# A Hymba-style layer in fp32 on one core: the S5 output matmuls as a task of their own, weights split three chunks ahead in the input projection, accumulators loaded one by one, and another root and other stores at the end

## The chip, the cores and the metric

The kernel runs on one core of a Trainium2 chip. The metric is the device time of one launch in microseconds (us); lower is better. Three runs of the kernel before took 2394.06 to 2394.51 us, with a median of 2394.2 us.

## The reference, cut to what matters

One layer is applied to 656 columns: 16 meta tokens, 512 prompt tokens and 8 streams of 16 sample tokens. Everything is fp32.

```python
hn = rmsnorm(x, g_mix);  proj = hn @ w_in              # 2048 -> 1024 (S5) + 1024 (pooling)
# S5: 64 groups of 16 channels, 64 complex states each
bu = einsum("gpn,blgn->blgp", b_bar, u);  h = scan(h*lam_bar + bu)
y  = einsum("gnp,blgp->blgn", c, h).real + d_skip * u
y  = gelu(y);  y = y * sigmoid(y @ w_glu)
# pooling: trailing means over 2/4/8/16 positions minus the token, times w_pool, times a scale
x  = x + concat([y, y_pool]) @ w_out
g, v = rmsnorm(x, g_ffn) @ w_up                        # 2048 -> 2 x 5632
x  = x + (gelu(causal_conv3(g)) * v) @ w_down          # 5632 -> 2048
out = rmsnorm(x, g_final)                              # and the final states of S5, pooling and conv
```

## The kernel before, in words

Activations lie channel-first: a tile has 128 channels on the partitions and up to 656 columns. Each fp32 product is made of three fp32r matmuls: the high part of a weight times the high and the low part of the activations, and the low part of the weight times the high part. Weights come from DRAM in chunks of four 128x128 tiles (`wraw`, issued by SP, L197). Each chunk is split into `wh` (a CAST on ACT) and `wl` (a subtraction on DVE), and PE then runs 24 main matmuls over it, each of 320 or 336 columns.

The stages in time, in us from the start of the span: input projection with the S5 and pooling work beside it (0 to about 475, with the first part of the output projection), the GLU matmuls (480 to 552), the rest of the output projection (to 650), the up projection as a Strassen-like scheme (to 1745), the down projection (to 2317), and its tail, which goes through the columns in two pieces of 384 and 256 (`TAIL`), the final RMSNorm and the stores of y.

S5 runs in eight blocks n of eight groups. `prep_b` and `prep_c` build the block's matrices (POOL, ACT and some small fp32 matmuls). `s5(n)` issues the input matmuls into PSUM tiles `vps`, copies them to `vt`, and does complex multiplications, rotations and two scans on DVE, with temporaries `pr` and `cr`. The last sum of a block on DVE is `vt<-pr,vt`. The output matmuls `yps` follow (`ymm`); they read `kst`, `cexp`, `ht` and `vt`. `s5_out(n)` then takes `yps` through gelu on ACT and DVE, stores the block to DRAM (`yg_d`), loads it again in another layout and splits it into the GLU's input `H`. The last block is needed by the first GLU row of weights whose input it is.

The order of instructions is not written by hand. One Python planner emits the instructions of all engines while it builds the program. The main line emits the main matmuls; after each of them `tick` gives background tasks (generators) a turn. A planner clock `E.now` is moved on by modelled matmul costs, and each other engine has such a clock (`Eng.clk`, moved on by a fixed and a per-element cost). A task yields until such clocks have reached what it waits for (`done`, `idle`, `until`), or until a flag of another task is set. On the chip each engine runs its own list in order, and semaphores hold the real dependences. So a planner cost that is off shows as a wait on the chip, because the engine's list is in the wrong order for it.

In the down projection, `feed` loads the hidden tiles (`hidb`, 320 KB each, L1528) and, at the start, the 16 residual tiles into `acc` (L1627). `evict_down` adds each finished PSUM tile (`md`, `me`) to `acc` on DVE. In the tail `fin_acc` adds the last PSUM tile, squares it on ACT, and sums the squares on POOL or DVE. `fin_norm` sums over the partitions with a matmul of ones, takes the reciprocal root as exp(-0.5 ln(s)), does a Newton step on DVE, multiplies, and stores (L1713).

Of the kernel before, what the change touches and what calls it, by code (L numbers as in the profile page):

```python
# [14 lines left out]
NFF = 44  # L15
# [94 lines left out]
class Eng:  # L110
# [3 lines left out]
    def __init__(self, E, eng, fixed, per, fast=None):  # L114
        self.E, self.eng, self.fixed, self.per, self.fast = E, eng, fixed, per, fast
        self.clk = 0.0

    def __getattr__(self, m):
# [12 lines left out]

        return call
# [27 lines left out]
class Emit:  # L160
    def __init__(self, tc, A):
        self.tc, self.nc, self.A = tc, tc.nc, A
        self.order = weight_order()
        self.wi = 0
        self.slot = 0
        self.bg = []
        self.raw = {}
        self.hl = {}
        self.nraw = 0
        self.nh = 0  # L170
        self.nchunk = len(self.order) // CH
# [103 lines left out]
def body(tc, A):  # L275
# [40 lines left out]
    with tc.manual_schedule():  # L316
# [5 lines left out]
        def w26():  # L322
            return sp.tile([128, NT], F32, tag="w26", name="w26", bufs=7)
# [222 lines left out]
        def prep_b(n):  # L546
# [20 lines left out]
            while gbusy[0]:  # L567
                yield
# [56 lines left out]
        def s5(n):  # L625
            q0 = 4 * n
            pr = sp.tile([128, 4, 2, 2, NB], F32, tag="pr", name="pr", bufs=1)
# [9 lines left out]
            S.copy(out=ht[:, :, 0, :, 33:41], in_=h0)  # L637
# [37 lines left out]
            gbusy[0] = False  # L675
# [4 lines left out]
            yield from V.idle()  # L680
            times1(vt[:, :, 1], m2c)
# [30 lines left out]
            yield from V.idle()  # L712
            yps = pps.tile([128, 2, 512], F32, tag="sy", name="yps", bufs=1)

            def ymm(q):
# [8 lines left out]
            times1(ht[:, :, 0], m2c)  # L724
            TT(ht[:, :, 1], vt[:, :, 1], pr[:, :, 0], ADD)
            yield from V.idle()
            yield from times2(ht, m1)
            TT(fl(od), fl(pr), fl(ev), ADD)
            yield from V.done(0.8)
            while not cready[0] > n:  # L730
                yield
            for q in range(4):
                ymm(q)
                if q % 2:
                    yield
# [45 lines left out]
        gbusy = [False]  # L781
# [36 lines left out]
        def s5_main():  # L818
            for n in range(NSSM):
                while bready[0] <= n:  # L820
                    yield
                gbusy[0] = True
# [782 lines left out]
        def feed():  # L1605
# [30 lines left out]

        def evict_down(n, t):
            av = half2(D["acc"][:, n])
# [28 lines left out]
        def fin_acc(n, o, w, p, last):  # L1667
# [5 lines left out]
            if last and n >= 14:  # L1673
                sqt.append(q)
                return
            if last:
                S.activation(out=av, in_=av, func=AF.Copy, scale=vcol(V_GFIN, n))
# [9 lines left out]
        def fin_norm(o, w, last):  # L1687
# [17 lines left out]
            for lo in cuts:  # L1705
                for m in range(lo, hi):
                    av = acc[:, m, o:o + w]
                    if last and m < 14:
                        TT(av, av, rw, MUL, G if m in (3, 6, 9, 12) else V)
                    else:  # L1710
                        STT(av, av, vcol(V_GFIN, m), rw, MUL, MUL)
                yield from V.done(0.1)
                SP.dma_start(out=A["y"][lo:hi, :, o:o + w].rearrange("n p c -> p n c"), in_=acc[:, lo:hi, o:o + w])  # L1713
# [6 lines left out]
        for half, (o, w) in enumerate(TAIL):  # L1720
            for ks, ns in tail_order(half):
# [15 lines left out]
                if half == 1 and ns == [12]:  # L1737
                    S.activation(out=dmy, in_=epst, func=AF.Ln)
            if half == 0:
                first = list(E.bg)  # L1740
# [18 lines left out]
    ("y", (16, 128, 640)), ("sst", (8, 128, 4, 2, 9)), ("pst", (8, 128, 15, 9)), ("cvo", (128, NFF, 2, 9)),  # L1759
# [58 lines left out]
def _gather(o):  # L1818
# [3 lines left out]
    y = o["y"].reshape(2048, 16, 40)  # L1822
# [25 lines left out]
```

## Time and profile before

| what | value |
|---|---|
| median of three runs | 2394.2 us |
| the profiled execution's own time | 2393.66 us |
| its span, first to last instruction | 2391.9 us, mean granted TensorE clock 0.991 |
| PE / PE weight loads busy | 2340.7 us (98%) / 2330.3 us (97%) |
| DVE / ACT / POOL busy | 1646.5 (69%) / 936.5 (39%) / 347.4 us (15%) |
| DMA | 265.93 MB, 111 GB/s on the mean |
| 165 to 270 us: PE, DVE, POOL busy of 105 us | 93.23, 87.42, 54.50 |
| 270 to 375 us | 94.57, 81.31, 40.34 |
| 375 to 480 us | 105.00, 74.02, 31.55 |

PE stands for TensorE's matmuls, DVE for VectorE, ACT for ScalarE, POOL for GpSimd and SP for SyncE, whose queue issues the transfers. The granted clock is a share of full speed: 1.00 is 2.4 GHz and 0.50 is 1.2 GHz.

### The profile page before, as it was taken

How to read it: one execution, taken by the hardware profiler on the slowest of the kernel's cores; microseconds unless marked ns; L12 is line 12 of the kernel's file. 1: busy time of each engine (PE TensorE's matmuls, PEld its weight loads, DVE VectorE, ACT ScalarE, POOL GpSimd, SP SyncE). 2: the span in 40 equal slices, each digit the busy share in tenths (PEclk: the TensorE clock that was granted, in tenths of full speed). 3: DMA queues.
4: the chain of work that ended last, by engine and by line, in shares of the span. 5: the costliest groups of instructions: out<-in, count | busy, mean ns of one | idle time of the engine just before them, and what ended most of it. 6: DMA issues, size and time to landing. Idle time of an engine off the chain costs nothing.

```text
span 2391.9 us, 41092 instructions
## 1 busy us (share of the span) xinstructions
PE 2340.7 (98%) x15824; PEld 2330.3 (97%) x15824; DVE 1646.5 (69%) x2725; ACT 936.5 (39%) x1631; POOL 347.4 (15%) x548
## 2 busy tenths in 40 slices
PE   9998989999999999999999999999999999999997
PEld 9997989999999999999999999999999999999997
DVE  7588677646798888888888888888853232422236
ACT  6233343335554444444444444444441221311124
POOL 5655433200000000000000000000000000000014
PEclk9999899999999999999999999999999999999999
DMA  5322235545533333333323333333473232422223
GB/s 187 113 79 82 81 113 178 159 137 162 165 104 106 92 108 91 99 106 97 108 89 101 100 100 106 92 102 95 115 243 103 86 124 72 135 75 76 72 84 110
DMA packets 151237, 265.93 MB, mean 111 GB/s; under 512 B 21120, under 2 KB 41728, under 8 KB 151040
## 3 DMA queue, kind: packets, MB, share of 16 engines
q1 hardware_dynamic: 144560, 248.10, 33.4%
q0 software_dynamic: 6336, 15.19, 2.2%
q8 instruction: 124, 2.03, 0.4%
q14 instruction: 73, 0.60, 0.1%
q10 hardware_dynamic: 144, 0.01, 0.0%
HBM read 225.10 MB, written 38.12 MB: 110 GB/s over the span
## 4 chain that ended last, share of the span: by engine, by line
PE 75%; DVE 2%; DMA 1%; issue 1%; ACT 0%; SPq 0%; DVEq 0%; POOL 0%; ACTq 0%; POOLq 0%
PE pu L157 44%; PE me L157 12%; PE md L157 12%; PE mm L157 5%; PE mf L157 2%; DVE acc L130 1%; DMA acc<-x_d 1%; DVE f L130 0%; DVE wl L130 0%; DMA hidb<-h_d 0%; DMA h_d<-f 0%; ACT wh L130 0%; DMA wr<-wup 0%; DVE XH L130 0%; SPq L1295 0%
## 5 line engine op out<-in xcount | busy, mean ns | idle before, releaser
L157 PE MATMUL pu<-XT,wh 128*128 128x320 f32 (+1 forms) x3696 | 823.7, 310 | 0.5 <-DVE f L130 0.5
L157 PEld LDWEIGHTS pu<-XT,wh 128*128 128x128 f32 x3696 | 620.3, 188 | 0.9 <-issue 0.7
L157 PE MATMUL pu<-XT,wl 128*128 128x320 f32 (+1 forms) x1848 | 572.2, 310 | 0.7 <-DVE wl L130 0.7
L130 ACT CAST wh<-wraw 128x512 fp32r<-128x512 f32 (+1 forms) x487 | 298.4, 617 | 588.8 <-PE md L157 219.9
L130 ACT CAST wh<-wr 128x512 fp32r<-128x512 f32 x434 | 269.2, 621 | 405.6 <-PE pu L157 252.4
L130 DVE TENSOR_TENSOR wl<-wraw,wh 128x512 fp32r<-128x512 f32 (+1 forms) x487 | 336.4, 705 | 93.3 <-ACT wh L130 89.9
L157 PE MATMUL mm<-H,wh 128*128 128x320 f32 (+2 forms) x1920 | 372.6, 316 | 9.2 <-ACT H L130 4.2
L157 PEld LDWEIGHTS pu<-XT,wl 128*128 128x128 f32 x1848 | 349.2, 189 | 1.4 <-DVE wl L130 1.4
L130 DVE TENSOR_TENSOR wl<-wr,wh 128x512 fp32r<-128x512 f32 x434 | 298.1, 687 | 72.7 <-ACT wh L130 66.9
L157 PEld LDWEIGHTS mm<-H,wh 128*128 128x128 f32 x1920 | 304.4, 190 | 12.2 <-issue 7.1
L157 PE MATMUL pu<-XH,wh 128*128 128x320 f32 (+1 forms) x1232 | 277.1, 310 | 0.0
L157 PE MATMUL mm<-H,wl 128*128 128x320 f32 x960 | 222.4, 313 | 0.0
L157 PEld LDWEIGHTS pu<-XH,wh 128*128 128x128 f32 x1232 | 207.1, 189 | 0.0
L157 PE MATMUL pu<-XH,wl 128*128 128x320 f32 (+1 forms) x616 | 190.3, 309 | 0.0
L130 DVE TENSOR_TENSOR acc<-md,acc 128x640 f32<-128x640 f32 (+2 forms) x48 | 34.0, 710 | 193.9 <-PE md L157 193.9
L157 PEld LDWEIGHTS mm<-H,wl 128*128 128x128 f32 x960 | 163.3, 190 | 0.5 <-DVE wl L130 0.4
L130 DVE TENSOR_TENSOR acc<-me,acc 128x640 f32<-128x640 f32 (+2 forms) x48 | 34.1, 711 | 186.5 <-PE me L157 186.5
L157 PE MATMUL me<-hidb,wh 128*128 128x320 f32 x832 | 157.0, 311 | 5.1 <-ACT wh L130 5.1
L157 PE MATMUL md<-hidb,wh 128*128 128x320 f32 x832 | 156.5, 310 | 0.0
L157 PEld LDWEIGHTS me<-hidb,wh 128*128 128x128 f32 x832 | 131.7, 189 | 5.3 <-ACT wh L130 5.3
L157 PEld LDWEIGHTS md<-hidb,wh 128*128 128x128 f32 x832 | 131.6, 189 | 0.0
L130 DVE TENSOR_TENSOR wr<-wr 128x512 f32<-128x512 f32 x172 | 118.4, 688 | 2.8
(241 smaller groups left out, 3248.6 us busy)
## 6 DMA issues: line engine op xcount, KB each, us to landing
wraw<-wts SPq DMA_DIRECT2D x323, 256.0 KB, 2.8
wr<-wup SPq DMA_DIRECT2D x260, 256.0 KB, 3.0
wraw<-wup SPq DMA_DIRECT2D x90, 256.0 KB, 2.7
h_d<-f POOLq DMA_DIRECT2D x44, 320.0 KB, 2.5
hidb<-h_d SPq DMA_DIRECT2D x30, 320.0 KB, 4.3
w<-yg_d SPq DMA_DIRECT2D x16, 328.0 KB, 3.2
w<-xr SPq DMA_DIRECT2D x16, 322.0 KB, 3.7
x_d<-w SPq DMA_DIRECT2D x16, 322.0 KB, 3.7
```

Of the source, the lines that this page charges most:

```text
L130: return f(*a, **k)
L157: return self.eng.matmul(out=out, lhsT=lhsT, rhs=rhs, start=start, stop=stop, **more)
```

## The change

- Planner: a DVE instruction costs 1.2 times as much in the planner while POOL's planner clock is ahead of it. The small S5 tiles `w26` have 6 buffers where there were 7.
- S5: `pr` has two buffers. The last sum of a block goes to `pr` where it went to `vt`, and the output matmuls read it there. They are now a task, `s5_y(n)`, and `s5_main` goes straight on to block n+1: its input matmuls may stand ahead of block n's output matmuls. The initial state is copied to `ht` only once block n-1's output matmuls are emitted. The flag `gbusy` becomes the counter `g_done`.
- Input projection: at row 3 of four, one more chunk is split, so that from there on weights are split three chunks ahead.
- Down projection: four residual tiles are loaded at the start, and the other twelve by a task, one each 6 us of planner time; `evict_down` is not emitted before its tile's load.
- Tail: `fin_acc` multiplies by `g_final` on ACT in both column pieces. The reciprocal root is a Sqrt on ACT (its table is loaded after the first piece by a small Sqrt), a DVE reciprocal and the Newton step. Each piece is multiplied by five DVE instructions (2, 4, 4, 4 and 2 tiles), none on POOL, and stored by five transfers to an output of its own, where a partition's data of one transfer lies together.

The diff, cut to its core:

```diff
-            self.clk = max(self.clk, self.E.now) + self.fixed + per * n
+            t = max(self.clk, self.E.now)
+            self.clk = t + (self.fixed + per * n) * (1.2 if self.rival and self.rival.clk > t else 1)
...
+        self.V.rival = self.G
...
-            return sp.tile([128, NT], F32, tag="w26", name="w26", bufs=7)
+            return sp.tile([128, NT], F32, tag="w26", name="w26", bufs=6)
...
-            while gbusy[0]:
+            while g_done[0] < n:
...
-            pr = sp.tile([128, 4, 2, 2, NB], F32, tag="pr", name="pr", bufs=1)
+            pr = sp.tile([128, 4, 2, 2, NB], F32, tag="pr", name="pr", bufs=2)
...
-            S.copy(out=ht[:, :, 0, :, 33:41], in_=h0)
...
+            while s5_done[0] < n:
+                yield
+            S.copy(out=ht[:, :, 0, :, 33:41], in_=h0)
             times1(vt[:, :, 1], m2c)
...
             yield from times2(ht, m1)
-            TT(fl(od), fl(pr), fl(ev), ADD)
-            yield from V.done(0.8)
+            TT(fl(pr), fl(pr), fl(ev), ADD)
+            E.spawn(s5_y(n, pr, st))
+
+        def s5_y(n, pr, st):
+            yield from V.done(1.5)
             while not cready[0] > n:
                 yield
+            yps = pps.tile([128, 2, 512], F32, tag="sy", name="yps", bufs=1)
             for q in range(4):
...
-                    T.matmul(out=ov[:, 1:4:2], lhsT=lhs, rhs=vt[:, q, 1:4:2, ri], start=False, stop=ri == 1)
+                    T.matmul(out=ov[:, 1:4:2], lhsT=lhs, rhs=pr[:, q, :, ri], start=False, stop=ri == 1)
...
+                if n == 2 and k == 3:
+                    E.split_hi()
+                    E.split_lo()
...
-            for g in range(16):
-                SP.dma_start(out=half2(D["acc"][:, g]), in_=x3_d[g])
-                if g % 4 == 3:
-                    yield 2
+            for g in range(4):
+                load_acc(g)
+                yield 2
+            E.spawn(rest_acc())
...
+        def rest_acc():
+            t = E.now
+            for g in range(4, 16):
+                yield from E.until(t + 10 + 6 * (g - 4))
+                load_acc(g)
+
         def evict_down(n, t):
+            while n not in accs:
+                E.tick(True)
...
-            S.activation(out=rw, in_=ps[:, 0:w], func=AF.Ln, bias=epst)
+            S.activation(out=rw, in_=ps[:, 0:w], func=AF.Sqrt, bias=epst)
...
-            S.activation(out=rw, in_=rw, func=AF.Exp, scale=-0.5)
-            S.clk += 2.6
-            yield from S.done()
+            yield from S.done(0.2)
+            V.reciprocal(out=rw, in_=rw)
             newton(rw, rw, aw, t2[:, 0:w])
...
-            cuts = (15, 14, 12, 10, 8, 6, 4, 2, 0) if last else tuple(range(14, -1, -2))
...
+            for lo in (14, 10, 6, 2, 0):
+                av = acc[:, lo:hi, o:o + w]
+                TT(av, av, rw.unsqueeze(1).to_broadcast([128, hi - lo, w]), MUL)
                 yield from V.done(0.1)
-                SP.dma_start(out=A["y"][lo:hi, :, o:o + w].rearrange("n p c -> p n c"), in_=acc[:, lo:hi, o:o + w])
+                SP.dma_start(out=A[f"y{int(last)}"][:, lo:hi], in_=av)
                 hi = lo
```

**Places in the order.** PE's list around the output matmuls of block 1 (`yps<-stk,kst` is the first of them; `vps` are the input matmuls of block 2; `mm` are main matmuls). Before:

```order
L157 MATMUL mm<-H_85,wl 128x336
L157 MATMUL yps<-stk,kst 128x164
L157 MATMUL yps<-ht,cexp 128x2x41
L157 MATMUL yps<-vt,cexp 128x2x41
...
L157 MATMUL mm<-H_85,wl 128x336
L157 MATMUL vps<-stk,gst 128x164 x4
L157 MATMUL mm<-H_85,wh 128x320 x2
```

The same place now:

```order
L159 MATMUL mm<-H_85,wl 128x336
L159 MATMUL vps<-stk,gst 128x164 x8
L159 MATMUL mm<-H_0_77,wh 128x320 x2
...
L159 MATMUL mm<-H_2_79,wl 128x336
L159 MATMUL yps<-stk,kst 128x164
L159 MATMUL yps<-ht,cexp 128x2x41
L159 MATMUL yps<-pr,cexp 128x2x41
```

The input matmuls of block 2 moved ahead of the output matmuls of block 1. Counted from the start of the program, 1014 main matmuls stood ahead of the first output matmul of block 1, and 1074 stand there now; for block 2 it is 1248 and 1284, for block 3 1464 and 1524, for block 7 2352 and 2370.

ACT's list around the output of block 7, the last one (`<-yps` reads the output matmuls, the ACTIVATE on a tile onto itself is first the tanh and then the scale by 0.5, `CAST H` splits the reloaded block). Before:

```order
L130 ACTIVATE w_5204<-yps 128x656
L130 CAST wh<-wraw 128x512
L130 ACTIVATE w_5204<-w_5204 128x656
L130 CAST wh<-wraw 128x512 x2
L130 ACTIVATE w_5203<-w_5203 128x656
L130 CAST wh<-wraw 128x512 x2
L130 CAST H_85<-w_5312 128x640
```

The same place now:

```order
L132 ACTIVATE w_5234<-yps 128x656
L132 CAST wh<-wraw 128x512 x2
L132 ACTIVATE w_5234<-w_5234 128x656
L132 CAST wh<-wraw 128x512
L132 ACTIVATE w_5233<-w_5233 128x656
L132 CAST wh<-wraw 128x512
L132 CAST H_85<-w_5348 128x640
```

One weight cast moved from behind the tanh to ahead of it, and the scale now has three casts ahead of it since `yps`, as before, but of chunks that are one later. On DVE the first gelu instruction on this block (a TENSOR_SCALAR) stood ahead of the eviction of the last pooling map (`w<-mm,w` x3) and stands behind it now.

SP's list where the accumulators are loaded. Before:

```order
L1528 DMA hidb<-h_d_150 128x640
L1627 DMA acc<-x_d_126 128x640
...
L1627 DMA acc<-x_d_133 128x640
L197 DMA wraw<-wts 128x512
L1627 DMA acc<-x_d_134 128x640
...
L1627 DMA acc<-x_d_141 128x640
L1528 DMA hidb<-h_d_151 128x640
```

The same place now:

```order
L1534 DMA hidb<-h_d_150 128x640
L1644 DMA acc<-x_d_126 128x640
L1644 DMA acc<-x_d_127 128x640
L200 DMA wraw<-wts 128x512
L1644 DMA acc<-x_d_128 128x640
L1644 DMA acc<-x_d_129 128x640
L1534 DMA hidb<-h_d_151 128x640
...
L1644 DMA acc<-x_d_130 128x640
```

Twelve of the sixteen loads moved behind the hidden tile `h_d_151`.

## Rows read from the trace of the kernel before

**Rows 1.** What PE waited for: times in us in total, count, longest.

```profile
PE yps L157 <- DVE vt L130: 16.5, 4, 6.2
PE me L157 <- ACT wh L130: 5.1, 1, 5.1
...
PE mm L157 <- DVE H L130: 3.3, 1, 3.3
```

**Rows 2.** Windows after five PE waits: PE PEld DVE ACT POOL, clock, DMA, GB/s.

```profile
185.40:192.40 7.00, 7.00 (x39) 7.00 (x40) 5.75 (x10) 0.00 (x0) 2.43 (x4) 0.66 0.45 113
238.30:245.30 7.00, 7.00 (x33) 7.00 (x33) 2.81 (x6) 0.73 (x1) 0.00 (x0) 0.54 0.30 92
287.20:294.20 7.00, 7.00 (x37) 6.94 (x38) 2.83 (x6) 1.31 (x2) 0.00 (x0) 0.62 0.40 112
323.70:330.70 7.00, 7.00 (x39) 7.00 (x40) 6.96 (x13) 1.64 (x4) 5.76 (x10) 0.79 0.74 212
1782.10:1789.10 7.00, 7.00 (x31) 7.00 (x32) 5.33 (x8) 4.26 (x7) 0.00 (x0) 0.61 0.90 307
```

**Rows 3.** Windows of S5 blocks 1 to 3, same columns.

```profile
149.20:185.30 36.10, 29.98 (x203) 28.97 (x201) 35.58 (x57) 11.46 (x23) 22.10 (x23) 0.97 0.25 69
185.30:197.50 12.20, 12.12 (x75) 12.12 (x76) 5.85 (x11) 2.03 (x6) 7.13 (x10) 0.80 0.27 67
197.50:238.30 40.80, 35.23 (x242) 34.65 (x240) 40.21 (x62) 16.32 (x33) 21.76 (x27) 1.00 0.33 95
238.30:251.20 12.90, 12.90 (x75) 12.90 (x76) 2.81 (x7) 2.77 (x7) 4.61 (x6) 0.75 0.16 50
251.20:287.20 36.00, 32.06 (x220) 31.49 (x218) 35.52 (x58) 14.77 (x30) 19.34 (x25) 0.98 0.34 95
```

**Rows 4.** Timeline of DVE, block 1: start, us, instruction.

```profile
172.82 0.16 DVE L130 TENSOR_TENSOR st<-pr 128x4 f32<-128x4 f32 x1
...
182.11 1.77 DVE L130 TENSOR_TENSOR pr<-pr,cr 128x656 f32<-128x656 f32 x1
183.91 1.42 DVE L130 TENSOR_TENSOR vt<-pr,vt 128x656 f32<-128x656 f32 x1
```

**Rows 5.** Groups of PE by form, 290 to 480 us: count, busy, mean ns.

```profile
L157 PE MATMUL vps<-stk,gst 128*128 128x164 f32 x64 | 10.5, 304 | 0.2 <-DVE H L130 0.2
```

**Rows 6.** Timeline of DVE and ACT around block 7's output.

```profile
477.67 0.84 DVE L130 TENSOR_TENSOR w<-w,w 128x656 f32<-128x656 f32 x1
...
480.90 0.95 DVE L130 TENSOR_TENSOR w<-mm,w 128x320 f32<-128x320 f32 x3 [2.39 <-PE mm L157]
...
483.24 0.75 ACT L130 ACTIVATE w<-w 128x656 f32<-128x656 f32 x1 [2.02 <-DVE w L130]
...
484.63 0.62 ACT L130 CAST wh<-wraw 128x512 fp32r<-128x512 f32 x1 [0.64 <-PE mm L157]
488.21 0.62 ACT L130 CAST wh<-wraw 128x512 fp32r<-128x512 f32 x1 [2.96 <-PE mm L157]
...
492.79 0.90 DVE L130 TENSOR_TENSOR H<-w,H 128x640 fp32r<-128x640 f32 x2 [3.23 <-ACT H L130]
```

**Rows 7.** Chain that ended last, 1750 to 1790 us: start, us, what.

```profile
1762.87 6.45 DMA acc<-x_d
...
1775.82 5.62 DMA hidb<-h_d
```

**Rows 8.** Timeline of the last 16 us.

```profile
2377.17 1.28 ACT L130 ACT_TABLE_LOAD   x1
...
2378.46 0.42 ACT L130 ACTIVATE f<-f 128x256 f32<-128x256 f32 x1
...
2380.29 1.35 DVE L130 SCALAR_TENSOR_TENSOR acc<-acc,vec,f 128x256 f32<-128x256 f32 x2
...
2381.56 5.01 DVE L130 TENSOR_TENSOR acc<-acc,f 128x256 f32<-128x256 f32 x10
```

**Rows 9.** Groups of DVE by form, 0 to 60 us.

```profile
L130 DVE RECIPROCAL pt<-pt 128x32 f32<-128x32 f32 x1 | 0.4, 352 | 4.2 <-POOL pt L130 4.2
```

More of the change, by code (lines that the diff above doesn't have):

```diff
@@ L116, in __init__ @@
         self.clk = 0.0
+        self.rival = None
     def __getattr__(self, m):
@@ L674, in s5 @@
                 gmm(q)
-            gbusy[0] = False
+            g_done[0] = n + 1
             yield from S.done(0.4)
@@ L712, in s5 @@
             yield from V.idle()
+            times1(ht[:, :, 0], m2c)
+            TT(ht[:, :, 1], vt[:, :, 1], pr[:, :, 0], ADD)
+            yield from V.idle()
+            yield from times2(ht, m1)
+            TT(fl(pr), fl(pr), fl(ev), ADD)
+            E.spawn(s5_y(n, pr, st))
+        def s5_y(n, pr, st):
+            yield from V.done(1.5)
+            while not cready[0] > n:
+                yield
             yps = pps.tile([128, 2, 512], F32, tag="sy", name="yps", bufs=1)
-            def ymm(q):
+            for q in range(4):
                 o = yps[:, q // 2, 164 * (q % 2):164 * (q % 2) + 164]
@@ L721, in ymm @@
                     T.matmul(out=ov[:, 0:4:2], lhsT=lhs, rhs=ht[:, q, :, ri], start=False, stop=False)
-                    T.matmul(out=ov[:, 1:4:2], lhsT=lhs, rhs=vt[:, q, 1:4:2, ri], start=False, stop=ri == 1)
[L724 to L727, printed above, removed]
-            TT(fl(od), fl(pr), fl(ev), ADD)
-            yield from V.done(0.8)
[L730 to L733, printed above, removed]
+                    T.matmul(out=ov[:, 1:4:2], lhsT=lhs, rhs=pr[:, q, :, ri], start=False, stop=ri == 1)
                 if q % 2:
@@ L779, in s5_out @@
             s5_out_done[0] += 1
-        gbusy = [False]
+        g_done = [0]
         cready = [0]
@@ L821, in s5_main @@
                     yield
-                gbusy[0] = True
                 yield from s5(n)
@@ L1635, in body, with load_acc @@
         E.spawn(feed())
+        def load_acc(g):
+            SP.dma_start(out=half2(D["acc"][:, g]), in_=x3_d[g])
+            accs.add(g)
+        accs = set()
+        def rest_acc():
[3 more added lines that the diff above has]
+                load_acc(g)
         def evict_down(n, t):
+            while n not in accs:
+                E.tick(True)
             av = half2(D["acc"][:, n])
@@ L1674, in fin_acc @@
                 sqt.append(q)
+                if n == 15:
+                    for m in (14, 15):
+                        am = acc[:, m, o:o + w]
+                        S.activation(out=am, in_=am, func=AF.Copy, scale=vcol(V_GFIN, m))
                 return
-            if last:
-                S.activation(out=av, in_=av, func=AF.Copy, scale=vcol(V_GFIN, n))
+            S.activation(out=av, in_=av, func=AF.Copy, scale=vcol(V_GFIN, n))
             yield from S.done()
@@ L1695, in fin_norm @@
             rw, aw = r[:, 0:w], a[:, 0:w]
-            S.activation(out=rw, in_=ps[:, 0:w], func=AF.Ln, bias=epst)
+            S.activation(out=rw, in_=ps[:, 0:w], func=AF.Sqrt, bias=epst)
             V.tensor_scalar(out=aw, in0=ps[:, 0:w], scalar1=1e-6, scalar2=None, op0=ADD)
-            S.activation(out=rw, in_=rw, func=AF.Exp, scale=-0.5)
-            S.clk += 2.6
-            yield from S.done()
+            yield from S.done(0.2)
+            V.reciprocal(out=rw, in_=rw)
             newton(rw, rw, aw, t2[:, 0:w])
             yield
-            cuts = (15, 14, 12, 10, 8, 6, 4, 2, 0) if last else tuple(range(14, -1, -2))
             hi = 16
[L1705 to L1711, printed above, removed]
+            for lo in (14, 10, 6, 2, 0):
+                av = acc[:, lo:hi, o:o + w]
+                TT(av, av, rw.unsqueeze(1).to_broadcast([128, hi - lo, w]), MUL)
                 yield from V.done(0.1)
-                SP.dma_start(out=A["y"][lo:hi, :, o:o + w].rearrange("n p c -> p n c"), in_=acc[:, lo:hi, o:o + w])
+                SP.dma_start(out=A[f"y{int(last)}"][:, lo:hi], in_=av)
                 hi = lo
@@ L1736, in body @@
                             E.spawn(fin_acc(n, o, w, pss[n], half == 1))
-                if half == 1 and ns == [12]:
-                    S.activation(out=dmy, in_=epst, func=AF.Ln)
             if half == 0:
+                S.activation(out=dmy, in_=epst, func=AF.Sqrt)
                 first = list(E.bg)
@@ L1758 @@
 _OUTS = [
-    ("y", (16, 128, 640)), ("sst", (8, 128, 4, 2, 9)), ("pst", (8, 128, 15, 9)), ("cvo", (128, NFF, 2, 9)),
+    ("y0", (128, 16, TAIL[0][1])), ("y1", (128, 16, TAIL[1][1])), ("sst", (8, 128, 4, 2, 9)), ("pst", (8, 128, 15, 9)), ("cvo", (128, NFF, 2, 9)),
 ]
@@ L1821, in _gather @@
     c = np.ascontiguousarray
-    y = o["y"].reshape(2048, 16, 40)
+    y = np.concatenate([o["y0"], o["y1"]], axis=2).transpose(1, 0, 2).reshape(2048, 16, 40)
     yp = c(y[:, :, 0:32].transpose(2, 1, 0).reshape(1, 512, 2048))
```

## The prediction

> **What bounds the kernel now.** I read the page first: PE is busy for 98% of the span, so only what PE waits for, and the time it spends at half clock behind a wait, can be won. The list of PE's waits comes next [rows 1]: 16.5 us for the last S5 sum (`yps <- vt`, four times), 5.1 us in the down projection for `wh`, 3.3 us for a pooling tile `H`. Then I read windows of 7 us from the end of each wait [rows 2], and the reader is to see the clock there: 0.66, 0.54, 0.62, 0.79 and 0.61, a mix of the two levels 1.2 and 2.4 GHz. PE had idled for 3 to 6 us before each. The loss is 7 us times (1 - clock): 2.4, 3.2, 2.7, 1.5 and 2.7 us. So a wait costs about its length and half as much again. In the S5 windows [rows 3] PE's idle time is 36.10 - 29.98 = 6.1, 40.80 - 35.23 = 5.6 and 36.00 - 32.06 = 3.9 us for blocks 1, 2 and 3, while DVE is busy for 35.58 of 36.10 us: there the DVE list sets the end, until PE is through the wait; in the 12.20 us after it DVE has only 5.85 us of work.
>
> **S5, blocks 1 to 3.** Now: 6.1 + 2.4 + 5.6 + 3.2 + 3.9 + 2.7 = 23.9 us. A main matmul costs PE (488.21 - 484.63) / 24 = 0.149 us: two weight casts that wait for PE lie one chunk of 24 matmuls apart [rows 6].
> Block 1: its output matmuls stand 60 main matmuls later (8.9 us) and behind block 2's input matmuls, 10.5 / 4 = 2.6 us a block [rows 5]: PE comes to them 11.5 us later. The last sum has also moved down DVE's list, behind some 5.9 us of pooling steps and splits, by the undisturbed length of such forms (a 656-column sum takes 0.84 us [rows 6]). Beside POOL the same width took 1.77 and 1.42 us [rows 4]. Lower price 5.9 us, upper double that. I take 7.4, a quarter more, because POOL is busy for 22.10 of 36.10 us [rows 3] and not each of these steps meets it. The wait left is 6.1 + 7.4 - 11.5 = 2.0 us, with some 1.5 at half clock.
> Block 2: when its sum was done, PE had lost 6.1 + 2.4 + 5.6 = 14.1 us. Against that, 36 main matmuls more (5.4 us, less 1.7 of small matmuls that went behind) and up to 12.20 - 5.85 = 6.35 us in which DVE stood idle because PE was late, and which a list that runs ahead can fill. DVE's list has 1.9 us more. 14.1 + 1.9 - 3.7 - 6.35 = 6.0 us of PE time lost up to there, block 1's 3.5 among it; behind that about 2.5 at half clock. Sum 8.5.
> Block 3: 14.1 + 3.2 + 3.9 = 21.2 us lost before; 3.2 us more DVE work, 10.8 us more PE work, and both idle stretches (6.35 and 12.90 - 2.81 = 10.1): nothing is left to wait for.
> So 23.9 becomes **8.5**, a gain of 15.4; bounds of what is left 0 (all steps undisturbed and well spread) and 24 (the price below). Block 0's wait (16.5 - 15.6 = 0.9 us) goes too, since its matmuls stand 30 main matmuls later: -0.8.
> The second `pr` buffer, the counter in place of the flag, and 6 small tiles for 7 cost nothing by themselves: they are allocations, and their price would be a wait inside the terms above.
>
> **The pooling tile.** 3.3 + 1.5 = 4.8 us [rows 1, 2]. It was late because DVE was behind when it came to it; with the backlog gone I keep 0.8: **-4.0**, bounds 0 and -4.8.
>
> **Weights split one chunk further ahead.** The instructions are the same, but `wh` has four buffers. The cast of a chunk three ahead waits for PE to leave the oldest, and it stands ahead of S5's work on ACT, which is in order. It matters at the end of S5, where the GLU waits for block 7's `H`. Before, nothing was to spare: the split was done at 492.79 + 0.90 = 493.7 [rows 6], and PE came to it at that time without a wait. Now: output matmuls 18 main matmuls later (2.7 us). The gelu's first DVE step stands behind the pooling eviction, which ends at 480.90 + 0.95 = 481.85. Then the step and its product, 0.5 + 0.84. The tanh stands behind the cast at 484.63, so it starts at 485.25 and ends at 486.0. The scale stands behind the cast at 488.21, so it starts at 488.83 and not at 483.24 [rows 6]: **5.6 us later**, and the stores, the load and the split behind it are the same. PE waits about 5.5 us and loses 2.5 at half clock, as after the other waits [rows 2]: **+8.0**, bounds 0 and +10.
>
> **Accumulators.** Before, 16 loads of 320 KB stood ahead of the hidden tile on SP. The chain shows them from 1762.87 to 1775.82, and then the hidden tile for 5.62 us [rows 7]; PE waited 5.1 us. With 4 ahead, 12/16 of 12.95, or 9.7 us, leave that path, more than the 5.1 awaited. **-7.8** with the clock (5.1 + 2.7). The twelve come later, one in 6 us: 320 KB in 6 us is 53 GB/s, where the chain's stretch moved over 300 (the last of [rows 2]). Bounds -7.8 and 0 (if another transfer is late next).
>
> **The end.** The table load (1.28 us) and the Exp (0.42) leave the path [rows 8]; the reciprocal joins it. The trace has one, of 32 columns: 0.352 us [rows 9]. Low bound 0.35, high 8 x 0.352 = 2.8 for 256 columns; a 4-column sum takes 0.16 [rows 4], so 0.192 / 28 = 6.9 ns a column, and I take 1.9 us. The Trainium skill ("VectorE: DVE Perf Modes", § First, the fixed hardware budget) says that the reciprocal is an iterative divide with a repeat count of 8; at eight times the pace of the 656-column sum that would be an estimate of 2.2 us, and the sum would be 0.3 us worse.
> Multiplying: STT 1.35 + TT 5.01 = 6.4 us on DVE with POOL's help [rows 8]; now 4096 columns at 0.84 / 656, 5.2 us. DVE is done about 1 us sooner, and the last store, of larger pieces, waits less for those before it: -2.5 at the end. In the second piece, the first piece's reciprocal (384 columns, 2.8 us by the same slope) and multiplications of 1536 columns (about 2 us each) stand on DVE between PSUM evictions; I charge 1.5 us of PE waits. Net **-1.0**, bounds -4 and +2.
>
> **Sum.** -15.4 - 0.8 - 4.0 + 8.0 - 7.8 - 1.0 = -21.0 us. The profiled execution took 2393.66 us (span 2391.9, 1.8 around it), 0.5 under the median of 2394.2. 2393.66 - 21.0 = 2372.7; I forecast **2372.5 us**.
>
> **Rivals.**
> A. *The end of S5 keeps up*: the GLU's wait does not appear, because casts and tanh meet in time. For it: ACT is not busy there. Against it: each step is in a list in order, and there was no slack. -21.0 - 8.0: about 2364.5, and 2356 if S5's waits vanish as well.
> B. *DVE stays the bound in S5.* The added steps cost double (rows 4 are near that): block 1 then waits 6.1 + 11.8 - 11.5 = 6.4 us, the backlog leaves no idle time to fill, and the 24 us stay: 2372.5 + 15.5 = 2388. The Trainium skill ("SBUF — State Buffer", § Who interferes with whom) has the rule for this: a DVE instruction with two SBUF inputs and a GpSimd instruction that reads SBUF lock each other out. By that rule, the sums of rows 4 would be stopped whole beside POOL. The trace agrees in part: such sums became longer there, but not by the whole length of POOL's work.
> C. *Slower: the accumulators come late.* From the fifth on, each tile must land before its first addition, and these come one per 9.7 us by PE's work (64 main matmuls or so). If the loads issue behind SP's blocked weight loads, DVE stops in order, with `wl` behind it. A late tile costs up to 6.5 us (half of 12.95, [rows 7]) and 2.7 of clock, 9.2 together. It decides at three late tiles: 2372.5 + 27.6 = 2400; five give 2418. Against: they are planned 6 us apart and so gain on the additions.
> D. *Nothing moves*: the three gains stand on three independent waits, so all three would have to come back elsewhere: 2390 to 2398.
>
> **How the numbers follow.** Forecast 0.50, A 0.20, B 0.20, C 0.04, D 0.06. Range 2356 to 2388: it takes in A with its bound, and B; C and D are outside. 0.2% is 4.8 us, about what a measurement can tell here. Faster (under 2389.4): forecast, A, B at most and a little of D, with B's upper part beyond the line: 0.86. Same 0.08, slower 0.06.
>
> **What would show it.** Right: the waits of `yps` at 6 us or less in all; no wait on `me` at the down projection's start, with the hidden tile landing before PE comes; a new wait of about 5.5 us of `mm <- H` near the GLU's end of its first row; a reciprocal of 256 columns at 1.9 us; the clock at 1.0 behind the old places. Wrong: `yps` waits above 12 us (B), a GLU without a wait (A), DVE waiting for `acc` loads (C).

## The result and the profile after

The changed kernel took 2380.28 us, the median of four runs (2379.2 to 2382.64), against 2394.22 us before: ratio 0.9943, 95% interval 0.9926 to 0.996. It is faster by 13.9 us, or 0.6%. The forecast was 2372.5 us with a range of 2356 to 2388, so the sign and the range held, and the gain came out at two thirds of the 21.7 us forecast. From the page of the changed kernel's profile (PE's busy time, its share and the count):

```profile
span 2378.7 us, 41101 instructions
...
PE 2335.2 (98%) x15824; PEld 2325.1 (98%) x15824; DVE 1657.4 (70%) x2709; ACT 944.0 (40%) x1644; POOL 353.4 (15%) x544
```

The span was 2391.9 us and is 2378.7 us: 13.2 us less. The list of what PE waited for (us in total, times, longest) has other names now [rows 1]:

```profile
PE vps L159 <- ACT vt L132: 9.2, 1, 9.2
PE mm L159 <- ACT H L132: 8.4, 2, 4.5
PE sv L159 <- DVE mp L132: 2.7, 1, 2.7
PE mm L159 <- DVE w L132: 2.0, 2, 1.8
PE mm L159 <- DVE H L132: 1.6, 3, 0.7
PE yps L159 <- DVE pr L132: 1.5, 1, 1.5
```

The waits of `yps` for `vt` and of `me` for `wh` are gone, and two new ones lead: 9.2 us of block 2's input matmuls for the ACT copy into `vt`, and two waits on `H`. Of the 8.4 us on `H`, the longest, 4.5, is at the very start of the program (4.2 before); the other, 3.8, is the GLU's. Three lines of the same list of the kernel before, for the smaller stretches (`mp` and `w` belong to the pooling):

```profile
PE mm L157 <- DVE w L130: 1.7, 2, 1.4
PE sv L157 <- DVE mp L130: 1.2, 1, 1.2
...
PE vps L157 <- DMA stk<-u_d: 1.1, 1, 1.1
```

The table sets the stages against each other. "Idle" is the sum of PE's gaps over 0.15 us in the stretch. "Half clock" is half of the time that PE worked at a granted clock of 0.50, which is what the lower level cost. Both are worked out from PE's timeline and the clock of each trace. Times are us from the span's start.

| stretch | before: idle + half clock | after | gain |
|---|---|---|---|
| S5 block 0 (100 to 140) | 1.8 + 0.0 | 0.0 + 0.0 | 1.8 |
| S5 blocks 1 to 3 (140 to 300) | 15.7 + 8.3 | 10.8 + 1.9 | 11.3 |
| S5 and pooling tiles (300 to 400) | 6.5 + 1.5 | 6.1 + 1.7 | 0.2 |
| before the GLU (460 to 500) | 0.3 + 0.0 | 5.2 + 4.6 | -9.5 |
| start of the down projection | 5.1 + 2.7 | 0.0 + 0.0 | 7.8 |
| tail, waits (2300 on) | 1.1 | 1.7 | -0.5 |
| from PE's last matmul to the end | 15.3 | 14.0 | 1.4 |

The gains add up to 12.5 of the 13.2 us. The rest is not in smaller gaps, which come to 0.1 us at most: the first matmul starts 0.3 us later than before, and PE's busy time, less the half clock, is 1.1 us shorter, for a reason that no run shows.

**Where S5 waits now.** The timeline of DVE and ACT in the wait, and the row of PE behind it:

```profile
183.44 0.81 DVE L132 TENSOR_TENSOR mp<-w,mp 128x642 fp32r<-128x642 f32 x1
...
184.18 0.77 DVE L132 TENSOR_TENSOR pc<-pz 128x600 f32<-128x600 f32 x1
...
187.05 0.73 DVE L132 TENSOR_TENSOR pd<-pc 128x560 f32<-128x560 f32 x1
...
188.99 0.48 DVE L132 TENSOR_TENSOR pd<-pc 128x320 f32<-128x320 f32 x1
...
190.78 0.84 DVE L132 TENSOR_TENSOR pr<-pr,vt 128x656 f32<-128x656 f32 x1
...
191.71 0.77 ACT L132 COPY vt<-vps 128x328 f32<-128x328 f32 x2 [13.02 <-DVE pr L132]
```

```profile
192.20 2.55 PE L159 MATMUL vps<-stk,gst 128*128 128x164 f32 x8 [9.21 <-ACT vt L132]
```

PE stops at 183.0 us, before the second half of block 2's input matmuls. Their PSUM tiles are free once ACT has copied them into `vt`, and that copy may start only when block 1's last sum (`pr<-pr,vt`, 190.78 us) has read `vt`. Pooling steps stand ahead of this sum on DVE (`mp`, `pc`, `pd` and a sum into `w`): 3.9 us of them, and 1.4 us of weight splits, lie inside the wait. So the wait that `yps` had on DVE is now a wait that `vps` has on DVE, by way of ACT. The prediction had looked for what is left of it at `yps` only.

**The GLU's wait.** The timeline of ACT:

```profile
469.78 0.62 ACT L132 CAST wh<-wraw 128x512 fp32r<-128x512 f32 x1 [3.41 <-PE mm L159]
470.30 0.75 ACT L132 ACTIVATE w<-w 128x656 f32<-128x656 f32 x1
473.30 0.62 ACT L132 CAST wh<-wraw 128x512 fp32r<-128x512 f32 x1 [2.24 <-PE mm L159]
473.82 0.75 ACT L132 ACTIVATE w<-w 128x656 f32<-128x656 f32 x1
476.83 0.62 ACT L132 CAST wh<-wraw 128x512 fp32r<-128x512 f32 x1 [2.26 <-PE mm L159]
481.90 0.83 ACT L132 CAST H<-w 128x640 fp32r<-128x640 f32 x2 [4.45 <-DMA w<-yg_d]
```

The tanh (470.30) starts behind the cast at 469.78, and the scale (473.82) behind the cast at 473.30; each of these casts had waited for PE. The split of `H` comes at 481.90, and PE had stood since 478.85. The windows of the two new waits and of what follows each (columns as in [rows 2]):

```profile
183.00:192.20 9.20, 0.00 (x0) 0.00 (x1) 9.06 (x17) 0.49 (x2) 0.10 (x1) 0.65 0.44 118
192.20:196.00 3.80, 3.80 (x14) 3.80 (x15) 1.72 (x4) 1.93 (x5) 0.13 (x1) 0.51 0.01 2
478.80:482.70 3.90, 0.06 (x2) 0.01 (x1) 0.03 (x1) 0.80 (x2) 0.00 (x0) 1.00 0.67 218
482.70:492.90 10.20, 9.08 (x31) 8.33 (x32) 4.23 (x9) 1.97 (x6) 0.00 (x0) 0.50 0.30 101
```

In the first wait the clock has already fallen before PE goes on, and only 3.8 us of work follow at 0.51. Behind the GLU's wait it is 0.50 for 10.2 us.

**Accumulators and the end.** SP's timeline (SPq is its queue) at the start of the down projection, and the last rows of the program:

```profile
1754.48 0.99 SPq L1644 DMA_DIRECT2D acc<-x_d  x2
1755.58 0.37 SPq L200 DMA_DIRECT2D wraw<-wts  x1
1755.99 0.90 SPq L1644 DMA_DIRECT2D acc<-x_d  x2
1756.94 1.09 SPq L1534 DMA_DIRECT2D hidb<-h_d  x2
```

```profile
2365.66 1.74 DVE L132 RECIPROCAL f<-f 128x256 f32<-128x256 f32 x1
2367.43 0.42 DVE L132 TENSOR_TENSOR f<-f 128x256 f32<-128x256 f32 x1
...
2368.81 4.70 DVE L132 TENSOR_TENSOR acc<-acc,f 128x512 f32<-128x512 f32 x5
2369.56 4.64 SPq L1730 DMA_DIRECT2D y<-acc  x5
```

Two hidden tiles are issued at 1756.94, right behind four accumulator loads, and PE does not wait. At the end the reciprocal of 256 columns took 1.74 us (forecast 1.9) and the five multiplications 4.70 us (forecast 5.2).

### The profile page after: what moved, and what is told of

Its sections match the earlier page's. It is cut to its first block, busy times and chain, and to the rows that moved or that the text cites. A ratio compares the mean times of both kernels' runs of the same rounds, so it can differ in the third digit from the quotient of the medians.

```text
span 2378.7 us, 41101 instructions
## 1 busy us (share of the span) xinstructions
PE 2335.2 (98%) x15824; PEld 2325.1 (98%) x15824; DVE 1657.4 (70%) x2709; ACT 944.0 (40%) x1644; POOL 353.4 (15%) x544
## 4 chain that ended last, share of the span: by engine, by line
PE 82%; DVE 2%; ACT 1%; issue 1%; POOL 0%; DMA 0%; SPq 0%; DVEq 0%; POOLq 0%; ACTq 0%
PE pu L159 45%; PE me L159 12%; PE md L159 12%; PE mm L159 9%; PE mf L159 2%; PE yps L159 1%; DVE f L132 1%; POOL ssq L132 0%; DVE wl L132 0%; DVE acc L132 0%; PE vps L159 0%; ACT f L132 0%; PE kp L159 0%; ACT wh L132 0%; DMA wr<-wup 0%
```

## The experiments

All twelve were compared with the kernel before on the same chip. Ratios to it, with 95% intervals, stand beside the medians; the changed kernel's is 0.9943 (0.9926 to 0.996). The chips differ, and so do the kernel before's medians there, 2392.9 to 2394.3 us, so medians of two experiments can lie 1 to 2 us apart for that alone. Differences of a few us against the changed kernel rest on the traces, each of one execution. "S5's stretch", "the pooling stretch" and "before the GLU" are rows of the table above, idle time + half clock.

**1. The half of `vt` that the last sum reads gets two buffers, and `pr` one.**

```diff
-        vt = sp.tile([128, 4, 4, 2, NB], F32, name="vt")
+        vo = sp.tile([128, 4, 2, 2, NB], F32, name="vo")
...
+            ve = sp.tile([128, 4, 2, 2, NB], F32, tag="ve", name="ve", bufs=2)
...
-            TT(fl(pr), fl(pr), fl(ev), ADD)
+            TT(fl(ev), fl(pr), fl(ev), ADD)
```

> The changed kernel with the input copies of an S5 block split into an even and an odd half; the even half, which the block's last sum reads, has two buffers, and pr has one (the sum is written to the even half in place). The order on PE, DVE, POOL and SP is the same. Theory 1: block 2's input matmuls waited 9.2 us because their copies had to wait for block 1's last sum to read the one buffer. Then this wait goes, PE comes to block 1's output matmuls at about 183 + 1.3 + 18 x 0.149 = 187 us, the last sum is still done at 191.6, and a wait of about 4.6 us stands there instead: about 2375.7 us. Theory 2: the backlog on DVE is the bound, wherever PE meets it: the wait moves as it is, 8 to 9 us at the output matmuls, 2379 to 2381 us.

Measured: 2381.76 us, 0.9952 (0.9937 to 0.9966), no faster than the changed kernel. From its list of waits:

```profile
PE yps L159 <- DVE ve L132: 8.8, 2, 4.8
PE mm L159 <- ACT H L132: 7.8, 2, 4.4
...
PE vps L159 <- ACT vo L648: 0.3, 1, 0.3
```

The wait at `vps` is gone (0.3 us), as theory 1 has it, and block 1's output matmuls wait 3.95 us, close to the 4.6 expected. But block 2's now wait 4.8 us (1.5 before). Idle and half clock between 140 and 300 us are 9.0 + 6.3 us, where the changed kernel has 10.8 + 1.9. So the buffer decides where PE meets the backlog. The backlog is DVE's, and here two waits of 4 to 5 us cost more at half clock than the one of 9 us. Theory 1 holds for the place and theory 2 for the time, 0.8 us over its range. (The split also makes ACT copy each input tile in two instructions instead of one; block 1's last sum is done at 192.4 us, 191.6 in the changed kernel.)

**2. Weights split two chunks ahead, as before the change.**

```diff
-                if n == 2 and k == 3:
-                    E.split_hi()
-                    E.split_lo()
```

> The changed kernel without the extra split at row 3 of the input projection: weights are split one chunk less far ahead, each list keeps its order otherwise. Theory 1 (the GLU's wait comes from weight casts that wait for PE ahead of block 7's gelu): each cast is released one chunk, 3.5 us, sooner; the wait on H falls from 5.0 to about 1.4 us, and its half clock with it: 2373 to 2376 us. Theory 2 (it comes from the output matmuls standing 18 main matmuls later and the eviction ahead of the gelu on DVE): the wait stays above 4 us, 2379 to 2381 us. If the extra chunk hid a wait for a weight split elsewhere, that wait shows, 1 to 3 us.

Measured: 2374.56 us, 0.9923 (0.9908 to 0.9938), 5.7 us under the changed kernel by the medians, 4.8 by the ratios and 7.4 by the spans of the two traces. Its waits:

```profile
PE mm L159 <- ACT H L132: 5.5, 2, 4.8
PE mm L159 <- DVE wl L132: 4.4, 2, 2.9
PE vps L159 <- ACT vt L132: 2.9, 1, 2.9
```

Before the GLU 1.4 us of idle time are left and no half clock (5.2 + 4.6 with three chunks): theory 1, to the expected 1.4 us. (The 4.8 us on `H` is the program's start.) The extra chunk does hide something: `wl` is now waited for twice, 4.4 us, just ahead of `vps`. But the wait at `vps` is shorter by 6.3 us, and S5's stretch has 8.5 + 3.2 us, 0.9 less than with the longer lead. This part of the change cost 5 to 7 us.

**3. The planner's price beside POOL back to 1.0.**

```diff
-(1.2 if self.rival and self.rival.clk > t else 1)
+(1.0 if self.rival and self.rival.clk > t else 1)
```

> The changed kernel with the planner's price of a DVE instruction beside POOL put back to 1.0. The output matmuls of blocks 1, 2 and 3 then stand behind 1026, 1230 and 1416 main matmuls where it was 1074, 1284 and 1524, that is 7, 8 and 16 us earlier, close to the kernel before (1014, 1248, 1464). Theory 1: the change's gain in S5 comes from this later place; without it the S5 waits with their half clock return to 20 to 26 us (from 12.6): 2388 to 2394 us. Theory 2: the gain comes from the task of its own and the second buffer, which let the next block's input matmuls go first; S5 stays at 10 to 15 us, 2378 to 2383 us.

Measured: 2379.56 us, 0.9941 (0.9925 to 0.9958), the same as the changed kernel. S5's stretch has 11.8 + 6.1 = 17.9 us, 5.3 more than with the price and 6.1 less than before the change; so both parts have a share in S5's gain, and neither theory's figure for S5 was met (20 to 26, 10 to 15). But the time does not move, because block 7's output matmuls stand behind 2274 main matmuls, 14 us sooner, and before the GLU only 1.3 us are idle, none of it for `H`, where the changed kernel has 5.2 + 4.6. What the price wins in blocks 1 to 3 it gives back at the GLU.

**4. The GLU's first three column tiles for each input tile, where it took two.** The weights' order and two loops change from `(0, 1)` to `(0, 1, 2)`; the third PSUM tile is the one of `yps`.

```diff
     for k in range(8):
-        for n in (0, 1):
+        for n in (0, 1, 2):
             o.append(("glu", k, n))
...
+        t = pps.tile([128, 2, 512], F32, tag="sy", name="yps", bufs=1)
+        pss.append([t[:, 0, :], t[:, 1, :]])
```

> The changed kernel with the GLU's first three column tiles taken together for each input tile (two before), the third in the PSUM tile that S5 has left: block 7 is then needed 7 x 6 = 42 main matmuls, 6.3 us, later. Theory 1: the wait on H of 5.0 us and the 4.6 us at half clock behind it cost their full length and go: about 2371 us. Theory 2: part of this was hidden or comes back when three column tiles finish at once (their gates need more of the six small buffers): 2375 to 2380 us.

Measured: 2373.22 us, 0.9916 (0.9901 to 0.9931), 7.1 us under the changed kernel by the medians, 6.5 by the ratios. Before the GLU 1.3 us are idle and no half clock is left, 8.4 us less by the trace: theory 1, whose 2371 us was 2 us too low.

**5. POOL kept quiet.** The building of `bexp` and `cexp` for S5 blocks 1 to 7 is left out, with the planner's clocks moved as if it were there.

```diff
-                TT(t1, bb(0), ff(ri), MUL, G)
+                GQ(t1, bb(0), ff(ri), MUL, n)
...
+        def GQ(o, a, b, op, n):
+            if n < 1:
+                return TT(o, a, b, op, G)
...
+            G.clk = max(G.clk, E.now) + G.fixed + G.per * k
```

> The changed kernel without the POOL instructions that build the matrices bexp and cexp of S5 blocks 1 to 7 (this part of the computation is left out, block 0's matrices are used again); the planner's clocks are moved on as if they were there, so the order on all engines is the same. They were 56 of POOL's 96 us between 136 and 300 us. Theory 1 (DVE falls behind in blocks 1 and 2 because its instructions are longer beside POOL's, about 0.5 us for each us of POOL): DVE is some 8 us sooner at block 1's last sum, the wait of 9.2 us at the input matmuls falls to 0 to 2 us and block 2's 1.5 us goes: 2369 to 2373 us. Theory 2 (DVE's list is too long or in the wrong order there, whatever POOL does): 7 us or more of waits stay, 2377 to 2381 us.

Measured: 2367.93 us, 0.9891 (0.9876 to 0.9905). Its waits, then its windows, and the same windows of the changed kernel (columns as in [rows 2]):

```profile
PE vps L159 <- ACT vt L132: 4.2, 1, 4.2
PE mm L159 <- DVE w L132: 2.1, 2, 1.8
...
PE sv L159 <- DVE mp L132: 0.9, 1, 0.9
```

```profile
136.80:183.00 46.20, 46.20 (x327) 45.74 (x326) 33.99 (x57) 17.61 (x35) 14.87 (x16) 1.00 0.29 76
...
sum 163.20, PE 158.98 PEld 157.03 DVE 126.09 ACT 67.52 POOL 40.03; mean PE 26.50 PEld 26.17 DVE 21.01 ACT 11.25 POOL 6.67
```

```profile
136.80:183.00 46.20, 46.20 (x326) 45.49 (x324) 36.12 (x53) 16.79 (x34) 28.84 (x36) 1.00 0.23 65
...
sum 163.20, PE 152.45 PEld 150.75 DVE 144.31 ACT 62.31 POOL 95.57; mean PE 25.41 PEld 25.13 DVE 24.05 ACT 10.38 POOL 15.93
```

With POOL at 40.0 us in place of 95.6, DVE was busy for 126.1 in place of 144.3 us in the same 163.2 us. But 18.2 / 55.6 = 0.33 is not the price of POOL, since DVE got further down its list in that time with POOL quiet. DVE's list is the same in both runs, 2709 instructions, so the same ones can be set side by side. The 214 that start between 136.8 and 300 us in the changed kernel keep DVE busy for 143.4 us there and for 118.9 us with POOL quiet, and POOL is busy for 93.1 and 39.2 us from the first of them to the last: 24.5 / 53.8 = 0.46 us of DVE for each us of POOL, near the 0.5 assumed. Late results of POOL were not what held the others up: between 136 and 300 us no engine waits for POOL in the changed kernel. S5's stretch fell from 12.6 to 5.9 us, and the pooling stretch (300 to 400) from 7.8 to 3.1 us. Theory 1 in its larger part: POOL's work stands behind some 11 us of PE's losses in these two stretches, and the time is 1 us better than its range. But 4.2 us at `vps` stay, where 0 to 2 were expected. Whose they are is open: POOL was not silent, but busy for 14.9 us (26.3 in the changed kernel) from 146 us to block 1's last sum, and the pooling steps still stand ahead of that sum. No run moves the sum alone ahead of them.

**6. The end of the kernel before.** `fin_acc`, `fin_norm`, the table load and the single output `y` are those of the kernel before.

```diff
-            S.activation(out=rw, in_=ps[:, 0:w], func=AF.Sqrt, bias=epst)
+            S.activation(out=rw, in_=ps[:, 0:w], func=AF.Ln, bias=epst)
```

> The changed kernel with the end of the kernel before: Ln and Exp, no reciprocal, g_final on DVE in the first column piece, multiplications shared with POOL, stores of one or two tiles. Theory 1: from the last main matmul to the end it takes 18.0 us again (16.3 in the changed kernel), and the first wait of 0.6 us in the second column piece goes: 2381 to 2382 us. Theory 2: the new end gains nothing once the first piece's reciprocal and long multiplications between the PSUM evictions are counted: 2379.5 to 2380.5 us.

Measured: 2382.66 us (2381.01 to 2384.69), 0.9952 (0.9935 to 0.9969). By the trace, from PE's last matmul to the end it takes 15.3 us (14.0), and the waits in the tail are 1.1 us (1.7): 0.8 us are lost by going back. (The 18.0 and 16.3 us of the theories count from the last main matmul.) The medians say 2.4, with spreads of over 3 us on both sides and intervals that overlap. So the sign is theory 1's by the traces alone, and the times do not settle the size.

**7. All sixteen accumulators at the start.**

```diff
-            for g in range(4):
+            for g in range(16):
                 load_acc(g)
-                yield 2
-            E.spawn(rest_acc())
+                if g % 4 == 3:
+                    yield 2
```

> The changed kernel with all 16 residual tiles loaded at the start of the down projection. Theory 1: they stand ahead of the hidden tile on SP and in the transfers; PE waits about 5 us there again and loses 2.7 us at half clock: 2387 to 2389 us. Theory 2: the hidden tile was late in the kernel before for another reason (its own store by POOL); the time stays at 2380 us.

Measured: 2386.49 us, 0.9969 (0.9957 to 0.998), 6.2 us more than the changed kernel. The old wait is back:

```profile
PE me L159 <- ACT wh L132: 4.1, 1, 4.1
```

4.1 us idle and 3.0 at half clock make 7.1 us. Theory 1, half a us under its 2387 to 2389.

**8. Experiments 2 and 4 together.**

> The GLU's first three column tiles together and weights split two chunks ahead. Theory 1: both take away the same wait before the GLU, so together they give little more than one of them: 2371 to 2373.5 us. Theory 2: the shorter lead gains mostly in S5 (its waits were 11.7 us with their clock, where the changed kernel has 12.6) or elsewhere, and the two add up: 2366 to 2369 us.

Measured: 2373.33 us, 0.9912 (0.9897 to 0.9926): the time of experiment 4 alone: together they give what one of them gives. Theory 1.

**9 to 11. Another price in the planner.** 9: 1.3 up to 150 us of planner time and 1.0 after; 10: that with experiment 4; 11: 1.3 up to 200 us with experiment 4.

```diff
-(1.2 if self.rival and self.rival.clk > t else 1)
+((1.3 if self.E.now < 150 else 1.0) if self.rival and self.rival.clk > t else 1)
```

> The changed kernel with the planner's price of a DVE instruction beside POOL at 1.3 up to 150 us of planner time and 1.0 after that. Block 2's input matmuls then stand behind 1104 main matmuls (1056 in the changed kernel), 7.1 us later; block 7's output matmuls behind 2340 (2370), 4.5 us sooner. Theory 1 (PE waits exactly by what the planner's place of S5's matmuls differs from when DVE is done): the wait of 9.2 us at block 2's input matmuls falls to about 2 us, with little or no half clock, and the wait on H before the GLU from 5.0 to about 0.5 us: 2380 - 9 - 9, about 2362 us, if blocks 3 to 6 stay without waits. Theory 2 (a backlog on DVE only moves on, as it did to block 2 when the even half got two buffers): 6 us or more of waits come up at blocks 2 to 4, 2368 to 2372 us.

> As before it, and the GLU's first three column tiles together. Theory 1: the wait on H is gone already, so this adds nothing: the same time as the run without it within 1 us, about 2362 us. Theory 2: the three column tiles cover the rest of the waits there: 1 to 2 us less.

> The price 1.3 up to 200 us of planner time, with the GLU's three column tiles together. Block 2's input matmuls stand behind 1128 main matmuls, blocks 2 and 3's output matmuls behind 1350 and 1596 (1284 and 1524 in the changed kernel), block 7's behind 2370 as in the changed kernel. Theory 1: block 1's wait is gone in full (10.7 us later than in the changed kernel) and block 2's too; the GLU's three column tiles hide block 7: 2360 to 2363 us. Theory 2 (the backlog moves on): waits of 6 us or more at blocks 2 to 4 or at the pooling tiles, 2367 us or more.

Measured: 2375.89, 2375.05 and 2379.09 us; 0.9922 (0.9907 to 0.9937), 0.9918 (0.9902 to 0.9935) and 0.9937 (0.9922 to 0.9952). The first of them waits for other things:

```profile
PE vps L159 <- ACT gst L132: 6.0, 2, 4.4
PE mm L159 <- ACT H L132: 4.2, 1, 4.2
PE sv L159 <- DVE mp L132: 3.6, 1, 3.6
```

The copies into `vt` are hardly waited for any more (1.2 us), and the GLU's wait fell to 1.3 us idle without half clock, as expected. But `vps` now waits 6.0 us for `gst`, its own weights, which ACT copies out of PSUM. ACT's timeline in that wait (PE goes on at 196.36 us):

```profile
192.30 0.73 ACT L132 CAST mp<-w 128x642 fp32r<-128x642 f32 x1 [9.60 <-DVE w L132]
...
195.73 1.06 ACT L132 COPY gst<-tp 128x512 f32<-128x512 f32 x2
```

The copy stands behind a cast that waited 9.60 us for a pooling sum on DVE. So this wait too is DVE's, by way of ACT. S5's stretch has 8.2 + 4.4, 8.8 + 2.5 and 11.8 + 3.4 us in the three runs, where the changed kernel has 10.8 + 1.9. For the mechanism that is theory 2 of experiments 9 and 11: the backlog moves on to another instruction. Experiment 9's time lies above both theories' ranges (2362, 2368 to 2372). Experiment 10 took 0.8 us less than 9, which is within the spread: the GLU's columns add nothing there, as its theory 1 had it, though not at 2362 us.

**12. Input matmuls held behind the output matmuls of the block before.**

```diff
+            while s5_done[0] < n:
+                yield
             gmm(0)
```

> The changed kernel with the input matmuls of a block held back until the output matmuls of the block before are emitted, as the order was in the kernel before; the output matmuls stay a task that the planner lets wait for DVE. They then stand behind 1152, 1398 and 1638 main matmuls for blocks 1 to 3 (1074, 1284 and 1524 in the changed kernel) and behind 2484 for block 7 (2370), 17 us later. Theory 1 (letting the next block's input matmuls go first is what keeps S5 short enough for the GLU; the waits in S5 come from the place alone): S5's waits of 12.6 us with their clock fall to 4 us or less, and the wait on H grows from 5.0 to some 20 us with half clock behind: 2380 - 9 + 15, 2384 to 2390 us. Theory 2 (the place of the input matmuls makes no difference to the sum): 2378 to 2382 us.

Measured: 2388.61 us, 0.9979 (0.997 to 0.9989). Its waits (4.8 of the 18.3 us are the program's start):

```profile
PE mm L159 <- ACT H L132: 18.3, 4, 12.4
PE mm L159 <- DVE H L132: 8.4, 4, 4.4
PE yps L159 <- DVE pr L132: 4.9, 2, 4.4
```

Theory 1 for the sum: the GLU's stretch has 18.4 + 4.7 = 23.1 us. S5's stretch has 8.7 + 5.0, not the 4 us expected; only the pooling stretch is better, at 1.3 us. With block 7's output matmuls 17 us later in the list, the GLU's stretch loses 13.3 us more than in the changed kernel (9.8). With this price in the planner, letting the next block's input matmuls go first is what keeps S5 short.

## Why the prediction was right, and where its terms were off

- **What bounds the kernel**: right. PE's waits, the longer ones with a stretch at half clock behind them, and the end behind PE's last matmul were what there was to win; PE's matmuls are the same 15824.
- **S5, blocks 1 to 3**: "23.9 becomes 8.5". It became 12.6 us (gain 11.3, forecast 15.4). The step that failed is the one for block 1, which set the output matmuls' place against the last sum and found 2.0 us. It did not ask who waits for the last sum's reading of `vt`: block 2's input matmuls, which now stand 18 main matmuls ahead of `yps`, wait for it through ACT's copies. The description of the change has them moved there.
  Even without that wait 2.0 us was too low: in experiment 1 the output matmuls wait 3.95 us. The price of the added DVE steps was not the error (the sum was done at 192.4 us there, and the forecast's 185.3 + 7.4 gives 192.7), but PE came at 188.5 us, where 179.2 + 11.5 gives 190.7; block 0's waits ahead of it, 1.8 us, were gone. In sum block 1 cost 9.2 + 1.9 = 11.1 us where the forecast had 3.5. Block 2's came out smaller, 1.5 us in place of 5.0, with PE already held up at block 1: up to block 2's sum PE had lost 12.6 us where the forecast had 6.0. Block 3 has no wait, as forecast. The forecast's own sign, `yps` waits at 6 us or less, came true at 1.5 us and still missed this, since the wait had changed its name. Experiment 1 shows that the place is the buffer's, and the time DVE's; experiment 5 that POOL stands behind about half of it.
- **The pooling tile**: -4.0 forecast, 0.2 measured. "With the backlog gone I keep 0.8" failed: the tile's own wait, on `H`, did fall from 3.3 us to 1.4, in two pieces, but in the same stretch `mp` went from 1.2 to 2.7 us and `w` from 1.4 to 1.8, and the half clock stayed (1.5, 1.7). The backlog was not gone at 300 us. With POOL quiet the stretch has 3.1 us in all.
- **Weights split one chunk further ahead**: +8.0 forecast, +9.5 measured (5.2 idle, 4.6 at half clock). Right in place and mechanism; the sizes met the sum partly by luck. The scale began 10.4 us ahead of PE's arrival before (483.24 to 493.7) and 5.0 us ahead now (473.82 to 478.85), 5.4 us later for the 5.6 forecast. But the stores, the load and the split behind it, taken as the same, were 1.6 us shorter, so the wait on `H` is 3.8 us and not 5.5. The half clock behind it took 4.6 us in place of 2.5, and in experiment 7 only 1.5 behind the same wait. Experiment 2 takes the casts' share away, 3.8 of the 5.2 us idle and the half clock with it; experiments 3 and 12 show the other cause, the place of block 7's output matmuls: with them 14 us sooner PE does not wait for `H` there at all, with them 17 us later it loses 23.1 us.
- **Accumulators**: -7.8 forecast, -7.8 measured; experiment 7 brings 7.1 of it back.
- **The end**: -1.0 forecast; 1.4 won behind PE's last matmul and 0.5 lost ahead of it, -0.9. The sum is right by luck: its two terms were 2.5 and 1.5, and both were about 1 us too large. The reciprocal's slope from the 32-column row (6.9 ns a column) gave 1.9 and 2.8 us; the rows show 1.74 and 2.54. The estimate worked out from the Trainium skill's repeat count of 8 ("VectorE: DVE Perf Modes", § First, the fixed hardware budget) was 2.2 us for 256 columns; the measured 1.74 us is below it. (At 0.84 / 656 us a column that estimate would be 2.6 us; 2.2 is about what the slope between the 4- and the 656-column sums gives.)
- **The rivals**: A was not the case, but experiments 2 and 4 made it the case and give 2374.6 and 2373.2 us, where A said 2364.5; most of the difference is what S5 and the pooling tiles kept. B was half the case: DVE did stay the bound in block 1. The rule that went with it, of an exclusive lock between DVE and GpSimd (the Trainium skill, "SBUF — State Buffer", § Who interferes with whom), agrees with the traces in part: quieting POOL shortens DVE's instructions. But DVE gained 0.46 us for each us of POOL, so POOL's time did not block DVE in full, and no run separates which of POOL's instructions did. C did not come: no accumulator was waited for.

The table's gains add up to 12.5 us where the sum said 21.0: 4.1 us are missing from S5, 3.8 from the pooling tile and 1.5 at the GLU, and block 0 gave 1.0 more, by luck: 1.1 of its 1.8 us was a wait of its input matmuls for a transfer (`stk<-u_d`) that the forecast did not name. The first two are of one kind: a backlog was taken as gone because the wait in which it had shown was covered. No run puts `w26` back to seven buffers, so its share is not shown.

## What to carry to other kernels

When a waiting step is moved down an engine's list, look at what has taken its place ahead of it, and follow that one's buffers too: a copy into a single buffer hands the old wait to the new front. A backlog on a second engine was not cured here by a second buffer or by still later places (experiments 1 and 9 to 11), since the next step that needed the engine met it; look for what makes its instructions long. And where work is split further ahead on an engine in order, the instruction that waits for a buffer holds up whatever stands behind it: ask what at the end of the stage needs that engine.

## What had not been expected of the hardware

One wait of 9.2 us cost less at half clock (1.9 us) than two waits of 4.0 and 4.8 us (6.3 us): in the long one the clock was at 0.50 from 185.7 to 195.95 us, for the most part while PE still stood, while behind each short one PE worked for 5 to 7 us at 0.50. In the trace's sums S5's stretch is 15.4 us with the two waits and 12.6 with the one; the medians are too close to show it. The price of a wait at half clock is not fixed even at one place: the GLU's wait of 3.8 us is followed by 10.2 us at 0.50 in the changed kernel, and in experiment 7 by 3.4 us only, so that the 10.2 us behind it have a mean clock of 0.83:

```profile
484.60:494.80 10.20, 8.74 (x47) 8.18 (x48) 5.18 (x11) 3.58 (x9) 0.00 (x0) 0.83 0.31 109
```

So some 3 us in the sum of a single trace can be chance. And DVE, which is slow beside POOL, did its rows in the wait at 183 to 192 us at undisturbed lengths (0.84 us for 656 columns), where POOL was busy for 0.10 us. This wait was a quiet stretch for DVE.
